# Two transformer blocks on one core: gate columns by TensorE, state steps on POOL, down products by token pair, norm turns emitted later

## The chip, the cores and the metric

The kernel runs on one core of a Trainium2 chip. The metric is device time in microseconds, the median of several runs. TensorE (PE in the profile) multiplies matrices and writes into PSUM; VectorE (DVE), ScalarE (ACT) and GpSimd (POOL) do the elementwise work; SyncE (SP) issues the transfers. Each engine carries out its own instructions in the order in which the program emitted them, and waits on semaphores for the others.

## The reference

Everything is float32, 512 tokens by 1024 features. A first block of two layers and then a second block of two layers are applied. What the change touches is cut out here:

```python
# first block, twice
h = rmsnorm(x, g_pre_mix[l]);  x = x + rmsnorm(token_mixer(h, ...), g_post_mix[l])
h = rmsnorm(x, g_pre_ffn[l]);  x = x + rmsnorm(conv_ffn(h, ...),    g_post_ffn[l])
# token_mixer: chunkwise mLSTM (4 heads, chunks of 128 tokens) beside sliding-window attention
log_i = gates[..., :4];  log_f = log_sigmoid(gates[..., 4:])     # gates: 8 columns per token
bc = cumsum(log_f in the chunk);  m, decays and weights from running maxima of log_i - bc
# conv_ffn: up to 2*2816 features, 3-tap causal convolution, silu(gate)*val, down to 1024
# second block, twice, with a context of 256 tokens
ret_x = bidirectional_retention(...)   # chunks of 128; per chunk: s = s * c_dec + k^T v, both ways
na_x, context_attention, pool_mixer, conv_ffn_2, all modulated by silu(c) @ w_mod
```

The mLSTM gates are 4 input and 4 forget values per token; the recurrence over tokens needs them as rows (one head's 512 tokens along the free axis), and the final division needs two results as columns again (tokens on partitions).

## The kernel before

All products of weights are made of three float32r matmuls (`mm3`, lines 444 to 449): each operand is split into a high part (`wh`, `nh`) and a remainder (`wl`, `nl`). Weights come as slabs of 512 KB through SP into a ring of three raw tiles, ScalarE casts the high part (line 385), VectorE subtracts the remainder (line 386), and five split slabs exist at a time (`NW`). `a_tiles` makes features by tokens (a slab is the stationary operand, up to 512 tokens move), `b_tiles` tokens by features (128 tokens are stationary, 512 weight columns move). Product banks in PSUM (`mm`) are four; four more (`ax`) serve transposes, scores and other small products.

**The order of the work** is laid down by a planned clock. The program is a generator that emits TensorE's products and yields their planned nanoseconds (`6 * 512 / 2.37`, or 1296, for six 512-column matmuls); everything else is put on a heap by `later(delay, fn)` (line 253) and is emitted when the planned clock has passed its due time, that is, at the next yield, in order of due time. Transposes and small products add to the clock themselves (`tr`, line 575: 110 or 60 ns). What is emitted in this order is what each engine runs; the real times follow from the semaphores. `Q` and the `D_` constants are such delays.

**A norm** (`Norm`, lines 124 to 191) goes token tile by token tile: square and sum on ScalarE (line 143), a root by VectorE (570) and a power on POOL (572), scaling of one half by VectorE (154) and of the other by ScalarE (155), then `turn` (159): four transposes each half by TensorE (577), the gain (168, 173, 175), and `put`: high part and remainder into `nh` and `nl` (187, 188). `D_TURN` is the delay from the scaling to the first turn.

**The first block's mixer** (`block1_mix`, line 1224) makes attention's queries (w1q), keys, values and gate columns (w1g), then the mLSTM's queries and keys (w1a, an `a_tiles` of four items, each evicted by ScalarE at line 1243 and finished by three taps on VectorE at line 1246; the last tap frees the bank), its values (w1v, which wants all four banks) and output gate (w1o). Between these products TensorE does the banks of the sliding-window attention (`swa_pair`, line 1027: scores, transposes, copies at 1075 and 1077, values `Q["sw3"]` after the transposes). The gates go their own way: `gates1` (line 892) at `Q["gates"]` after w1g; `gates2` writes them element by element to HBM (912), `gates3` reads them back as rows (920), `gates4` makes the cumulative sum (935), `stab` the running maximum and four more rows (940 to 944), `fin` writes five rows to HBM (950), `cols` reads two of them back as columns, element by element (957), `ends` takes an exponential (962). The mLSTM heads wait for these.

**The FFN** (`ffn`, line 644) is cut into parts by `PARTS1` and `PARTS2`: for each part the up products with convolution, then `down` (line 505): all token tiles for output half 0, then all for half 1. A token is complete when both halves of the last part are in; `b1_sink` then takes the root, updates x and starts the next norm. `down` begins with two tokens and leaves out the last two of the part's feature tiles until both have got the others. Modulation sums of the second block (`mod`, line 795) run on VectorE while an FFN allows it; `keep` (862) writes four gate rows to HBM by 4-byte elements.

**The second block.** `ctx_in` and `x_layer` make the projections, neighbourhood attention, pooling and retention. In `x_layer` the states of the four chunks are chained both ways (line 1861): a step (1353) is a multiply (1357) and an add (1358) over 64 partitions; f steps go to VectorE and b steps to POOL, in turn, the two halves lying in the same tiles. `ret_chunk` (line 1470) then does a chunk: scaling of q (1477), transposes, scores, products with the state. `ctx_attn` (line 1540) normalises its scores on POOL (593) and transposes them `Q["cx2"]` later.

## Time and profile before

| | us |
|---|---|
| median of 3 runs (2811.86 to 2814.61) | 2812.58 |
| the profiled execution, its own time | 2813.32 |
| its span, first to last instruction | 2811.5 |
| TensorE busy | 2705.4 (96%) |
| VectorE busy | 1895.9 (67%) |
| ScalarE busy | 1167.0 (42%) |
| POOL busy | 572.0 (20%) |

The profile is of one execution. A line of it names the source line of the kernel (L447), the engine, the operation and the tiles, "out<-in". A wait is an engine's idle time ahead of an instruction, put down to the semaphore that came last; where two instructions of the other engine end together, the name can be the neighbour's. A matmul's bar is longer than its share of the pipeline: two that follow each other overlap. PEclk is the granted share of TensorE's full clock.

### The profile page before, as it was taken

The numbers are of one execution on the slowest core, as the hardware profiler recorded it, in microseconds if no ns is written. First come the engines' busy times: TensorE is split into PE (matmuls) and PEld (weight loads), VectorE is DVE, ScalarE is ACT, GpSimd is POOL, SyncE is SP. The second block draws the span as 40 slices with busy tenths as digits, with TensorE's granted clock in tenths as the row PEclk, the third lists the DMA queues.
The fourth block names the chain that finished last, engine by engine and source line by source line (L and its number), as shares of the span: only waits on it lengthen the run. The fifth ranks groups of instructions, "written<-read, shape, count | busy, mean of one in ns | idle before, by whom it ended". The sixth has DMA issues, their size and how long they took to land. (4 is left out here: it accounts for less than half of the span.)

```text
span 2811.5 us, 38854 instructions
## 1 busy us (share of the span) xinstructions
PE 2705.4 (96%) x14526; PEld 2291.8 (82%) x14526; DVE 1895.9 (67%) x3414; ACT 1167.0 (42%) x2098; POOL 572.0 (20%) x616
## 2 busy tenths in 40 slices
PE   8899999998999999999999999999999999999998
PEld 6678888876788887788788888888888888888887
DVE  6767777777668678857657787778646556664544
ACT  4555332445554323555443633223336442442433
POOL 2222000042230000234153220221102335201011
PEclk9999999999999999999999999999999999999999
DMA  5633444425334464333332243333513322333332
GB/s 166 89 90 124 148 153 140 145 77 86 91 112 153 149 124 158 123 118 113 105 92 82 87 139 117 105 117 109 87 49 98 116 73 73 97 118 100 98 98 68
DMA packets 135804, 308.22 MB, mean 110 GB/s; under 512 B 38024, under 2 KB 44040, under 8 KB 135616
## 3 DMA queue, kind: packets, MB, share of 16 engines
q1 hardware_dynamic: 135040, 304.69, 37.3%
q8 instruction: 115, 1.88, 0.3%
q10 hardware_dynamic: 576, 1.05, 0.1%
q14 instruction: 73, 0.60, 0.1%
HBM read 303.44 MB, written 2.24 MB: 109 GB/s over the span
## 5 line engine op out<-in xcount | busy, mean ns | idle before, releaser
L385 ACT CAST wh<-wr 128x1024 fp32r<-128x1024 f32 (+2 forms) x455 | 461.3, 1015 | 578.4 <-PE mm L449 259.6
L447 PE MATMUL mm<-nh,wh 128*128 128x512 f32 (+1 forms) x1776 | 671.6, 378 | 3.6 <-DVE nh L187 3.6
L448 PE MATMUL mm<-nl,wh 128*128 128x512 f32 (+1 forms) x1776 | 666.9, 375 | 0.9 <-POOL nl L188 0.4
L449 PE MATMUL mm<-nh,wl 128*128 128x512 f32 (+1 forms) x1776 | 665.9, 375 | 0.0
L386 DVE TENSOR_TENSOR wl<-wr,wh 128x1024 fp32r<-128x1024 f32 (+2 forms) x455 | 572.3, 1263 | 112.5 <-ACT wh L385 112.1
L617 DVE SCALAR_TENSOR_TENSOR u<-mm,vec,u 128x511 f32<-128x511 f32 (+2 forms) x440 | 305.9, 695 | 234.6 <-ACT u L612 163.5
L447 PE MATMUL mm<-wh,u 128*128 128x512 f32 (+1 forms) x1176 | 460.5, 392 | 2.1 <-ACT u L632 1.9
L448 PE MATMUL mm<-wl,u 128*128 128x512 f32 (+1 forms) x1176 | 454.7, 387 | 2.6 <-DVE wl L386 2.4
L449 PE MATMUL mm<-wh,u 128*128 128x512 f32 (+1 forms) x1176 | 454.4, 386 | 2.2 <-DVE u L633 1.5
L447 PEld LDWEIGHTS mm<-nh,wh 128*128 128x128 f32 x1776 | 336.6, 190 | 66.3 <-issue 4.8
L449 PEld LDWEIGHTS mm<-nh,wl 128*128 128x128 f32 x1776 | 336.0, 189 | 60.4
L448 PEld LDWEIGHTS mm<-nl,wh 128*128 128x128 f32 x1776 | 336.6, 190 | 58.1 <-DVE nl L188 1.0
L447 PEld LDWEIGHTS mm<-wh,u 128*128 128x128 f32 x1176 | 221.9, 189 | 46.8 <-ACT u L632 2.7
L449 PEld LDWEIGHTS mm<-wh,u 128*128 128x128 f32 x1176 | 221.6, 188 | 46.0 <-DVE u L633 3.5
L448 PEld LDWEIGHTS mm<-wl,u 128*128 128x128 f32 x1176 | 222.0, 189 | 45.3 <-DVE wl L386 5.0
L447 PE MATMUL mm<-wh,nh 128*128 128x384 f32 (+2 forms) x512 | 191.1, 373 | 17.2 <-DVE t L934 10.8
L577 PE MATMUL ax<-ident,u 128*128 128x128 f32 x930 | 137.4, 283 | 50.6 <-DVE u L154 18.3
L449 PE MATMUL mm<-wh,nl 128*128 128x384 f32 (+2 forms) x512 | 182.0, 355 | 1.5 <-POOL nl L188 1.5
L448 PE MATMUL mm<-wl,nh 128*128 128x384 f32 (+2 forms) x512 | 181.7, 355 | 0.0
L577 PEld LDWEIGHTS ax<-ident,u 128*128 128x128 f32 x930 | 108.5, 144 | 80.9 <-issue 25.0
L737 POOL TENSOR_TENSOR x<-x,u 128x512 f32<-128x512 f32 x64 | 103.2, 1613 | 342.6 <-DVE u L736 341.4
L572 POOL TENSOR_TENSOR t<-t,mhalf 128x1 f32<-128x1 f32 (+2 forms) x76 | 63.3, 835 | 508.1 <-DVE t L570 507.8
(248 smaller groups left out, 3703.9 us busy)
## 6 DMA issues: line engine op xcount, KB each, us to landing
wr<-in_up_dram SPq DMA_DIRECT2D x176, 512.0 KB
mrow<-in_wmod_dram SPq DMA_DIRECT2D x192, 256.0 KB
wr<-in_dn_dram SPq DMA_DIRECT2D x88, 512.0 KB
wr<-in_wo_dram SPq DMA_DIRECT2D x56, 512.0 KB
wr<-in_w2b_dram SPq DMA_DIRECT2D x56, 384.0 KB
wr<-in_w2a_dram SPq DMA_DIRECT2D x39, 512.0 KB
nab<-in_nab_dram SPq DMA_DIRECT2D x36, 128.0 KB
wr<-in_w1q_dram SPq DMA_DIRECT2D x8, 512.0 KB
```

What stands on the lines that cost most here:

```text
L385: nc.scalar.copy(h[:, :n], raw[:, :n])
L386: s.wlo[i] = lambda: nc.vector.tensor_sub(lo[:, :n], raw[:, :n], h[:, :n].bitcast(F32))
L447: mm(ps, ah, bh, start=first, stop=False)
L448: mm(ps, ah, bl, start=False, stop=False)
L449: mm(ps, al, bh, start=False, stop=last)
L572: nc.gpsimd.tensor_tensor(out=r, in0=e, in1=s.mhalf[:, :n], op=ALU.pow)
L577: s.nc.tensor.transpose(out, in_, s.ident[:p, :p])
L617: nc.vector.scalar_tensor_tensor(out=c[:, o], in0=ps[:, i], scalar=w[q], in1=c[:, o], op0=ALU.mult, op1=ALU.add)
L737: eng.tensor_add(x[:, c], x[:, c], o)
```

## The change

Six things, each to be found in the diff:

- `Norm.scale` adds `D_MORE` = 1300 to the delay of both turns, except for the first norm of the kernel.
- `PARTS1` of the first layer becomes (0, 8, 14, 18, 22), as the second layer's is. The last part's down products of both layers of the first block go through a new `down_both`: both halves for tokens 0 and 1, then both for tokens 2 and 3, with all four slabs held.
- `Q["sw3"]` goes from 1250 to 2100 and `Q["cx2"]` from 2160 to 3200.
- `keep` issues its four transfers 4000 ns apart.
- `gates2` turns the gate columns into rows by eight transposes on TensorE, and goes on with what `gates4` did; `fin` writes three rows to HBM where it wrote five, and makes the columns by eight transposes.
- In `x_layer` all six state steps go to POOL, the backward ones first.

```diff
--- before.py
+++ after.py
@@ -29,6 +29,7 @@
 D_SQ = 1080
 D_RSQ = 990
 D_TURN = 1575
+D_MORE = 1300
 D_EV = 1500
 NW = 5
 ALIGNED = ("wh", "wl", "nh", "nl")
@@ -44,11 +45,11 @@
 D_W = 3080
 D_PUMP = 2500
 D_LO = 3000
-PARTS1 = ((0, 8, 16, 22), (0, 8, 14, 18, 22))
+PARTS1 = ((0, 8, 14, 18, 22), (0, 8, 14, 18, 22))
 PARTS2 = ((0, 4, 8, 12, 16, 22), (0, 8, 16, 22))
 CB = ((0, 0), (8, 1), (24, 1), (32, 2))
 NR = 3
-Q = {"swa": 2600, "ctx": 612, "na": 1218, "ret": 6600, "mod": 19000, "mod0": 30000.0, "cn": 18000, "gates": 16000, "fill": 11520, "na1": 1600, "na2": 6253, "na3": 2116, "sw1": 1400, "sw2": 3135, "sw3": 1250, "cx1": 1080, "cx2": 2160, "cx3": 1557}
+Q = {"swa": 2600, "ctx": 612, "na": 1218, "ret": 6600, "mod": 19000, "mod0": 30000.0, "cn": 18000, "gates": 16000, "fill": 11520, "na1": 1600, "na2": 6253, "na3": 2116, "sw1": 1400, "sw2": 3135, "sw3": 2100, "cx1": 1080, "cx2": 3200, "cx3": 1557}
 
 VEC = {}
 NVEC = 0
@@ -125,6 +126,7 @@
     def __init__(n, s, xs, gcol, bcol=None):
         n.s, n.xs, n.g, n.b = s, xs, gcol, bcol
         n.t = len(xs) * P
+        n.first = s.now == 0
         n.done = 0
         n.hh = n.hl = None
 
@@ -153,8 +155,9 @@
         hn = [s.u(), s.u()]
         nc.vector.tensor_scalar(out=hn[0], in0=x[:, :512], scalar1=r, scalar2=None, op0=ALU.mult)
         nc.scalar.activation(hn[1], x[:, 512:], AF.Copy, scale=r)
-        s.later(D_TURN, lambda: n.turn(i, 0, hn))
-        s.later(D_TURN + 426, lambda: n.turn(i, 1, hn))
+        late = 0 if n.first else D_MORE
+        s.later(D_TURN + late, lambda: n.turn(i, 0, hn))
+        s.later(D_TURN + late + 426, lambda: n.turn(i, 1, hn))
 
     def turn(n, i, h, hn):
         s, nc = n.s, n.s.nc
@@ -535,6 +538,35 @@
                     s.drop_w()
             s.done(ev(t, pss[t]))
 
+    def down_both(s, keys, act, ready, ev):
+        ws = [[], []]
+        nk = 2 * len(keys[0])
+        order = [(h, t) for q in ((0, 1), (2, 3)) for h in range(2) for t in q]
+        pss = {}
+
+        def part(n, k0, k1):
+            h, t = order[n]
+            if n not in pss:
+                yield from s.until(lambda: s.free > 0)
+                pss[n] = s.mm()
+            for k in range(k0, k1):
+                if len(ws[h]) <= k // 2:
+                    ws[h].append(s.load_w(keys[h][k // 2]))
+                wh, wl = ws[h][k // 2]
+                c = slice(k % 2 * 512, (k % 2 + 1) * 512)
+                yield from s.until(lambda: ready(k, 0))
+                s.mm3(pss[n], act(k, 0, t), (wh[:, c], wl[:, c]), k == 0, k == nk - 1)
+                if k % 2:
+                    yield 6 * 512 / 2.37
+                    if t == 3:
+                        s.drop_w()
+        for n, (h, t) in enumerate(order):
+            if n == 0:
+                yield from part(0, 0, nk - 2)
+                yield from part(1, 0, nk - 2)
+            yield from part(n, nk - 2 if n < 2 else 0, nk)
+            s.done(ev(h, t, pss[n]))
+
     def down(s, keys, act, ready, tiles, ev):
         w = []
         nk = 2 * len(keys)
@@ -667,6 +699,11 @@
                 c = slice(t * P, (t + 1) * P)
                 return h[:, c], lo[:, c]
             tiles = [(gi, t) for gi, n in enumerate(groups) for t in range(n.t // P)]
+            if up == "up1" and i == np_ - 1:
+                allow(False)
+                keys = [[(dn, (l, h, j)) for j in range(f0 // 2, f1 // 2)] for h in range(2)]
+                yield from s.down_both(keys, act, lambda k, gi, f0=f0: (f0 + k, gi) in g, sinks[0][1])
+                return
             for half in range(2):
                 if half and i == np_ - 1:
                     allow(False)
@@ -861,11 +898,16 @@
 
             def keep():
                 gd = s.dram([2, 2, D], "mgate")
-                for w in range(2):
-                    for i in range(2):
-                        o = (3 * i + 2) * 8
-                        nc.sync.dma_start(gd[w, i].rearrange("(j p) -> p j", p=P), md[:, w, o:o + 8])
-                s.mgate[l] = gd
+
+                def one(n):
+                    w, i = n // 2, n % 2
+                    o = (3 * i + 2) * 8
+                    nc.sync.dma_start(gd[w, i].rearrange("(j p) -> p j", p=P), md[:, w, o:o + 8])
+                    if n < 3:
+                        s.later(4000, lambda: one(n + 1))
+                    else:
+                        s.mgate[l] = gd
+                one(0)
             s.later(1200, keep)
 
         def begin(n):
@@ -902,27 +944,18 @@
         nc.scalar.activation(tmp, tmp, AF.Exp, scale=-1.0)
         nc.scalar.activation(tmp, tmp, AF.Ln, bias=s.one)
         nc.vector.scalar_tensor_tensor(out=lf3, in0=g3[:, :, 4:], scalar=0.0, in1=t3, op0=ALU.min, op1=ALU.subtract)
-        gd = s.dram([8, 512], "grow")
-        s.later(6000, lambda: s.gates2(g3, lf3, gd, got))
-
-    def gates2(s, g3, lf3, gd, got):
-        nc = s.nc
-        for i, src in enumerate((g3, lf3)):
+        s.later(7400, lambda: s.gates2(g3, lf3, got))
+
+    def gates2(s, g3, lf3, got):
+        nc = s.nc
+        rows = []
+        for src in (g3, lf3):
+            ps = s.ax()
             for t in range(NT):
-                nc.sync.dma_start(gd[i * 4:i * 4 + 4, t * P:(t + 1) * P].rearrange("h p -> p h"), src[:, t, :4])
-        s.later(3000, lambda: s.gates3(gd, got))
-
-    def gates3(s, gd, got):
-        nc = s.nc
-        rows = []
-        for i in range(2):
+                s.tr(ps[:4, t * P:(t + 1) * P], src[:, t, :4])
             r = s.u((4, 512))
-            nc.sync.dma_start(r, gd[i * 4:i * 4 + 4])
+            nc.vector.tensor_copy(r, ps[:4, :])
             rows.append(r)
-        s.later(2800, lambda: s.gates4(rows, got))
-
-    def gates4(s, rows, got):
-        nc = s.nc
         li, lfr = rows
         b, bm, m = [s.u((4, 512)) for _ in range(3)]
         a, wi, ws, d0 = li, lfr, b, bm
@@ -942,24 +975,20 @@
             nc.vector.tensor_add(bm, b, m)
             nc.vector.tensor_sub(wi3, mi[:, :NT].unsqueeze(2).to_broadcast([4, NT, P]), m3)
             nc.vector.tensor_sub(ws3, a3, m3[:, :, P - 1:].to_broadcast([4, NT, P]))
-            s.later(2600, fin)
+            s.later(4200, fin)
 
         def fin():
-            gr = s.dram([5, 4, 512], "gfin")
-            for i, x in enumerate((bm, a, m, wi, ws)):
+            gr = s.dram([3, 4, 512], "gfin")
+            for i, x in enumerate((m, wi, ws)):
                 nc.sync.dma_start(gr[i], x)
-            s.later(2600, lambda: cols(gr))
-
-        def cols(gr):
+            ps = s.ax()
+            for i, x in enumerate((bm, a)):
+                for c in range(NT):
+                    o = i * 16 + c * 4
+                    s.tr(ps[:, o:o + 4], x[:, c * P:(c + 1) * P])
             co = s.ti(32)
-            for i in range(2):
-                for c in range(NT):
-                    nc.sync.dma_start(co[:, i * 16 + c * 4:i * 16 + c * 4 + 4],
-                                      gr[i, :, c * P:(c + 1) * P].rearrange("h p -> p h"))
-            s.later(2800, lambda: ends(gr, co))
-
-        def ends(gr, co):
-            nc.scalar.activation(co[:, :16], co[:, :16], AF.Exp, scale=-1.0)
+            nc.scalar.activation(co[:, :16], ps[:, :16], AF.Exp, scale=-1.0)
+            nc.vector.tensor_copy(co[:, 16:], ps[:, 16:32])
             got["gates"] = (co[:, :16], gr, co[:, 16:])
         s.later(1800, stab)
 
@@ -1099,7 +1128,7 @@
         dec = [None] * 4
 
         def bring(hp):
-            for src, dst in ((4, wsb), (3, wib)):
+            for src, dst in ((2, wsb), (1, wib)):
                 w = s.u()
                 for i in range(2):
                     nc.sync.dma_start(w[i * 64:i * 64 + 64, :], gr[src, hp * 2 + i].partition_broadcast(64))
@@ -1108,7 +1137,7 @@
         def bring_m(hp):
             for i in range(2):
                 w = s.u()
-                nc.sync.dma_start(w, gr[2, hp * 2 + i].partition_broadcast(P))
+                nc.sync.dma_start(w, gr[0, hp * 2 + i].partition_broadcast(P))
                 dec[hp * 2 + i] = w
             s.later(2800, lambda: mask(hp))
 
@@ -1859,10 +1888,10 @@
         gn = s.gn_row(l)
         yield from s.in_b(l, 0, norm, s.tok(rq, True))
         yield from s.until(lambda: len(kv) == NT)
+        for d in range(NT - 1, 0, -1):
+            s.step(nc.gpsimd, rc, b, st[d - 1], st[d])
         for c in range(NT - 1):
-            s.step(nc.vector, rc, f, st[c + 1], st[c])
-            d = NT - 1 - c
-            s.step(nc.gpsimd, rc, b, st[d - 1], st[d])
+            s.step(nc.gpsimd, rc, f, st[c + 1], st[c])
 
         def ev_gate(t, ps):
             gate[t] = s.ret_gate1(ps, gn)
```

## Rows read from the trace of the kernel before

**Rows 1.** The page's busy time by engine, and the clock of the core.
```profile
PE 2705.4 (96%) x14526; PEld 2291.8 (82%) x14526; DVE 1895.9 (67%) x3414; ACT 1167.0 (42%) x2098; POOL 572.0 (20%) x616
...
core 0: 2811.5 us, clock 0.989
```
**Rows 2.** TensorE's waits, whole span: us in total, times, longest.
```profile
PE ax L577 <- DVE u L154: 18.3, 12, 7.0
PE mm L447 <- DVE t L934: 10.8, 2, 5.4
PE ax L577 <- DVE u L1477: 10.3, 2, 5.2
PE mm L447 <- DVE nh L187: 9.8, 4, 3.3
PE ax L589 <- ACT u L1075: 7.3, 6, 3.0
...
PE ax L577 <- ACT u L155: 3.7, 2, 2.1
```
**Rows 3.** Timeline of 1481 to 1500, VectorE and POOL: start, us, instruction.
```profile
1487.51 0.95 DVE L1381 TENSOR_TENSOR u<-u,cos 128x384 f32<-128x384 f32 x1
...
1491.79 0.55 DVE L1357 TENSOR_TENSOR u<-u,t 64x384 f32<-64x384 f32 x1 [2.09 <-POOL u L1358]
...
1498.79 1.81 DVE L1477 TENSOR_TENSOR u<-u,t 128x384 f32<-128x384 f32 x2
...
1481.24 6.80 POOL L1379 TENSOR_TENSOR u<-u,sin 128x192 f32<-128x192 f32 x8 [4.92 <-ACT u L1715]
1489.84 0.83 POOL L1357 TENSOR_TENSOR u<-u,t 64x384 f32<-64x384 f32 x1 [1.80 <-DVE u L1358]
1490.75 1.00 POOL L1358 TENSOR_TENSOR u<-u,u 64x384 f32<-64x384 f32 x1
...
1497.40 2.32 POOL L1358 TENSOR_TENSOR u<-u,u 64x384 f32<-64x384 f32 x1
```
**Rows 4.** Timeline of 1494 to 1519, TensorE.
```profile
1500.19 1.54 PE L577 MATMUL ax<-ident,u 128*128 128x128 f32 x6 [5.13 <-DVE u L1477]
...
1508.30 0.42 PE L447 MATMUL mm<-wh,nh 128*128 128x384 f32 x1
...
1513.24 0.82 PE L577 MATMUL ax<-ident,u 128*128 128x128 f32 x6
...
1518.60 0.48 PE L447 MATMUL mm<-wh,u 128*128 128x512 f32 x1
```
**Rows 5.** Stretches: length, busy time (instructions) of each engine, clock, DMA share, GB/s.
```profile
185.00:205.00 20.00, 20.00 (x90) 16.53 (x89) 10.10 (x13) 8.44 (x16) 5.49 (x5) 1.00 0.42 132
226.00:250.00 24.00, 20.18 (x141) 19.15 (x139) 16.22 (x25) 9.07 (x20) 6.96 (x6) 0.86 0.33 99
596.00:610.00 14.00, 8.35 (x36) 6.05 (x35) 11.90 (x21) 10.37 (x22) 8.40 (x8) 0.88 0.12 32
1096.00:1172.00 76.00, 72.33 (x315) 58.63 (x315) 59.13 (x106) 26.75 (x39) 1.53 (x2) 1.00 0.41 136
```
**Rows 6.** Timeline of 98 to 114, lines of TensorE and VectorE.
```profile
101.73 0.77 PE L447 MATMUL mm<-wh,nh 128*128 128x512 f32 x1 [5.38 <-DVE t L934]
...
98.20 0.75 DVE L1246 SCALAR_TENSOR_TENSOR u<-mm,vec,u 128x511 f32<-128x511 f32 x1 [2.22 <-ACT u L1243]
100.84 0.74 DVE L1246 SCALAR_TENSOR_TENSOR u<-mm,vec,u 128x509 f32<-128x509 f32 x1
103.69 1.21 DVE L935 TENSOR_TENSOR_SCAN u<-u,u 4x512 f32<-4x512 f32 x1 [2.11 <-DMA u<-grow]
109.68 1.91 DVE L940 TENSOR_TENSOR_SCAN u<-u,u 4x512 f32<-4x512 f32 x1
112.91 0.67 DVE L944 TENSOR_TENSOR u<-u,u 4x512 f32<-4x512 f32 x1
```
**Rows 7.** TensorE's waits from 1225 to 1270, in the first `ctx_in`.
```profile
PE ax L577 <- POOL u L593: 5.1, 4, 2.2
```

More of the change, by code (lines that the diff above doesn't have):

```diff
@@ L904, in gates1 @@
         nc.vector.scalar_tensor_tensor(out=lf3, in0=g3[:, :, 4:], scalar=0.0, in1=t3, op0=ALU.min, op1=ALU.subtract)
-        gd = s.dram([8, 512], "grow")
-        s.later(6000, lambda: s.gates2(g3, lf3, gd, got))
-    def gates2(s, g3, lf3, gd, got):
-        nc = s.nc
-        for i, src in enumerate((g3, lf3)):
-            for t in range(NT):
-                nc.sync.dma_start(gd[i * 4:i * 4 + 4, t * P:(t + 1) * P].rearrange("h p -> p h"), src[:, t, :4])
-        s.later(3000, lambda: s.gates3(gd, got))
-    def gates3(s, gd, got):
+        s.later(7400, lambda: s.gates2(g3, lf3, got))
+    def gates2(s, g3, lf3, got):
         nc = s.nc
         rows = []
-        for i in range(2):
+        for src in (g3, lf3):
+            ps = s.ax()
+            for t in range(NT):
+                s.tr(ps[:4, t * P:(t + 1) * P], src[:, t, :4])
             r = s.u((4, 512))
-            nc.sync.dma_start(r, gd[i * 4:i * 4 + 4])
+            nc.vector.tensor_copy(r, ps[:4, :])
             rows.append(r)
-        s.later(2800, lambda: s.gates4(rows, got))
-    def gates4(s, rows, got):
-        nc = s.nc
         li, lfr = rows
```

## The prediction

> **What bounds the kernel now.** I read the page's first part and the clock first. TensorE is busy for 2705 of 2811.5 us at a granted clock of 0.989 [rows 1]: about 106 us of idle time and a few slow stretches are all there is to win unless matmuls go, and none go (the reference's products all stay). So only what TensorE waits for matters. The list of its waits [rows 2] is to be read as places: transposes ("ax") of the norms waiting for the scaled token (L154), 18.3 us over 12, of which 7.0 is the kernel's start and 11.3 the other eleven; L155, the same on ScalarE, 3.7; weights products waiting for a normalised token (nh), 9.8 over 4; L1477, the retention chunk, 10.3 in two equal parts; L934, 10.8 in two; L1075, 7.3 over 6. Every layer pays these again, so the two big pairs are one cause each. The sum is made against the profiled execution's own 2813.32 us (span 2811.5 and 1.8 around it); the median of the runs shown is 0.74 lower.
>
> **State steps on POOL (line 1862).** Today the steps alternate: a VectorE step waits 2.09 us for a POOL step on the same tile and the other way round, and only behind the third VectorE step does L1477 come, at 1498.79 [rows 3]; TensorE has stood 5.13 us [rows 4]. Without the steps VectorE has L1381 done at 1488.46 [rows 3]; two adds of a like size, one weight remainder (about 1.2) and L1477 (1.81) follow, so about 1493.4, before TensorE gets there (1500.19 less 5.13). The wait goes. Behind it TensorE ran slower: from the transposes at 1500.19 to the first matmul after the products at 1508.30 is 8.11 us, the next chunk's same instructions take 5.36 (1513.24 to 1518.60) [rows 4]; 2.75 more. Per layer 7.9, for two 15.8; I take off 1.0 for VectorE, which then stands nearer to the chain: **-14.8**. What is late next? POOL does six steps in a row, 0.83 and 1.00 each, from about 1488.0 when its rotary work ends [rows 3]. The backward steps come first, so the state of chunk 0 is there at about 1493.7, and the products, over at 1508.30 today, want it no earlier than about 1498. Every f step lies ahead of its chunk too. POOL's bound is 0.83 and 2.32 a step [rows 3]: third step at 1497.5, still in time.
> That 2.32 us add began while VectorE ran two operations with both inputs in SBUF. The Trainium skill (SBUF — State Buffer, "Who interferes with whom") says that such an operation and a GpSimd one which reads SBUF lock each other out for a whole instruction. The trace agrees: 2.32 against 1.00. By that rule all six steps run at the long price and the state is ready at 1497.5, so it changes neither sign nor sum here.
>
> **Norm turns one step later (D_MORE).** The program is emitted by a planned clock that moves in steps of 1296 (six 512-column products); 1575 falls on the second step, 2875 on the third. So each turn is passed by six more products, 6 x 20/90 = 1.33 us [rows 5], if there are any. Thirteen waits for L154 and L155 (the start excepted) come to 15.0 us, mean 1.15 [rows 2]; one is at the first layer's end, below. For the twelve others I take 0.95 each, 11.4. At both ends of the mixers (226 to 250 in the first layer, idle 3.8 [rows 5], and the second alike) the last token has no products left to hide behind; but its root no longer queues behind the stores of the token ahead: 1.0 each. **-13.4**; bounds 4 (half of the waits only move to nh) and 15.0, and 3 us more if the slow clock of 0.86 at 226 goes.
>
> **Down products by token pair, parts (8, 14, 18, 22).** In the first layer's last down stage token 0 was complete 42 products before the end; now it is 60 of 96, 13.3 us. The 42 were 9.3 us, so its chain has 4.0 us more. TensorE idles 14.0 - 8.35 = 5.65 us there and the clock is 0.88, worth 1.7 [rows 5]; less 4.0 the wait is 1.65, and I leave 2.0 of the 7.4, as tokens 2 and 3 are complete only 12 and 0 products ahead: **-5.4** (0 to 7.4). Against it, the smaller part has twelve products, not 24, before it needs its last activation. The second layer has these very parts, and from 1096 to 1172, over the starts of its last two down stages, TensorE idles 3.7 us [rows 5]: **+3.7**. The eight added partial sums are VectorE work of some 0.75 us each (a tap's price [rows 6]) within one part's up stage and down stage, hidden while VectorE is busy 67% [rows 1]. In the second layer nothing waits for its tokens: 0. Four weight tiles of five are held at once; they were split a tile ahead, and if they weren't, a wait for a remainder is about 1.3 us each. That the modulation sums pause one half earlier costs nothing, since their rows are fetched only in the second block.
>
> **ctx_attn (cx2).** Its four waits for POOL's L593 are 5.1 us [rows 7]; one step later, 1.1 remains, and I give back 1.5 to weights that come no sooner: **-2.4** (0 to 5.1).
>
> **Gates and sw3.** SP loses 16 element-wise transfers and 4 whole ones a layer, and spreads the four of `keep`. No wait of TensorE in the list is put down to a transfer, so 0; were a weight's transfer late behind them, it would be a gain. sw3 takes the value products past one more step: of the 7.3 us for L1075 I take 4.5. But the order on VectorE matters. TensorE stands 5.38 us at 101.73, put down to L934; by the code it is the fourth bank of the value product that it wants, which the third tap (L1246, 100.84 to 101.58) frees; L934 only stands beside it [rows 6]. The change does not remove that. By the planned clock (the yields, transposes and scores of the code added up since w1g) gates1 comes 17288 ns after the w1g products; 7400 more is 24688, inside the point (24622 to 26355) at which a bank's scores and transposes are emitted, and that point comes ahead of the last w1a item's own taps. So gates2 stands before them on VectorE: two copies of 0.75, scan 1.21, a sub of 0.67 and a small copy, some 3.5 us, where VectorE was idle 2.22 ahead of 98.20; +1.3. And the block `stab`, due 1800 after it, falls before the third tap, due 2194 after. It runs from 109.68 to 113.58, 3.9 us [rows 6], and then stands in front of TensorE. The bank waits, and behind that product all of TensorE's queue. The eight transposes of gates2 lie inside this wait; the eight of `fin` don't, 1.1 (six take 0.82 [rows 4]); its exp and 16-column copy are small and awaited only by the mLSTM heads, much later. 6.3 per layer, 12.6 for two, less 4.5: **+8.1**. Bounds: -3 (stab after the tap) and +12 (two more slow windows).
>
> **Sum.** -14.8 - 13.4 - 5.4 + 3.7 - 2.4 + 8.1 = -24.2; 2813.3 - 24.2 - 0.7 = **2788.4 us**.
>
> **Rivals.** (a) *The gates don't stand in the way*: the tap goes first, or another link frees TensorE. The 8.1 becomes about zero: 2780. For it speaks the list, which names L934; against it the planned clock, which gives today's order of VectorE row by row. (b) *Waits that only move*: a turn that comes later finds TensorE at nh or at a weight remainder, because the last token's chain is no shorter. Half of the 13.4 + 5.4 + 2.4 is lost, 10.6: about 2799; all of it, 2809, no measurable change. For it: nh has 9.8 us over 4 already. (c) *Slower*: of the ten norms' 34 tokens each turn is put 1.33 us later, also where the consumer is next in line. Without the 13.4 the sum is -10.8; from 13 such tokens on, at 1.33 each, it is past 2813.3 + 5.6 less the 0.7, and with all 34 it is 2847. Against it: only 4 nh waits in the whole list, so few turns are next in line. (d) *It doesn't do what it says*: 1300 would move nothing if it fell within one step; it doesn't, as worked out.
>
> **Numbers.** Forecast 0.52 (its own range 2779 to 2797), (a) 0.20, (b) 0.22 (0.07 of it within 0.2%), (c) 0.05, (d) 0.01. About 0.2%, 5.6 us, is what a measurement of this kernel can tell from no change. Faster 0.87, same 0.08, slower 0.05. The range 2773 to 2806 takes in the forecast, (a) with two slow windows gone, and most of (b).
>
> **What would show it.** L1477 gone from the waits, six POOL steps in a row from 1488, and the chunk's instructions at the 5.36 us of today's second chunk: the first term right. The first value product of each mixer waiting about 8.5 us, for something behind L944: the gates right; 5.4 or less: rival (a). At the first layer's end idle of about 2 in place of 5.65, and new waits of 3.7 together before its two last down stages. L154 and L155 together under 4 us apart from the start, with nh at 9.8 or less; nh above it is (b) or (c). A wait of the chunk's products for POOL, or for a weight in the pair-wise stage, would prove me wrong there.

## The result and the profile after

The changed kernel takes **2839.6 us** (median of 4 runs, 2836.5 to 2845.8) against 2812.7 before: ratio 1.0098, 95% interval 1.0078 to 1.0117. It is slower by 27 us where 24 less were forecast. The profiled execution is the longest of the four, 2845.8, 6 us above the median, and what is read from it below is of that one execution. Its first page lines and its list of TensorE's waits (engine, operation and line; releaser; us in total, times, longest) answer to [rows 1, 2]:

```profile
core 0: 2844.0 us, clock 0.981
PE 2718.3 (96%) x14558; PEld 2302.0 (81%) x14558; DVE 1899.9 (67%) x3416; ACT 1166.5 (41%) x2098; POOL 587.6 (21%) x628
```

```profile
PE mm L450 <- DVE u L1275: 16.1, 2, 8.1
PE ax L609 <- DVE u L156: 13.0, 7, 6.9
PE mm L450 <- DVE nh L190: 12.0, 4, 5.4
PE mm L450 <- ACT u L664: 10.8, 4, 7.8
PE ax L609 <- DVE u L1506: 10.2, 4, 3.3
PE mm L450 <- DVE u L649: 9.5, 2, 8.7
PE mm L451 <- DVE wl L389: 8.8, 9, 2.7
...
PE ax L613 <- DVE u L1517: 3.8, 2, 1.9
...
PE mm L452 <- DVE wl L389: 2.8, 1, 2.8
PE ax L609 <- POOL u L625: 2.7, 4, 0.9
```

Idle time rose from 106.1 to 125.7 us (span less busy), and busy time by 12.9 with only 32 small transposes more, whose bars are 3.9 us together: behind the longer waits the granted clock is at half of its full rate for longer (0.50 in every microsecond from 1517 to 1523, behind the retention's waits; 0.981 over the span, where 0.989 was). Line numbers have moved (L154 is L156, L187 L190, L386 L389, L632 L664, L617 L649, L593 L625, L1246 L1275, L1477 L1506, L1488 L1517). Read group by group: the norms' L156 fell from 18.3 to 13.0 [rows 2], but L190 rose from 9.8 to 12.0, and the waits for weight remainders (L389) from 4.7 in four to 11.6 in ten. The retention did not lose its 10.3; it has 14.0, now with L1517. The first value product has 16.1 where it had 10.8. Two waits are new: 7.84 for L664 and 8.74 for L649. The largest, from the timelines of the changed kernel (start, us, engine, line, operation, shapes, [idle before it <- releaser]):

```profile
106.23 0.76 PE L450 MATMUL mm<-wh,nh 128*128 128x512 f32 x1 [8.06 <-DVE u L1275]
610.95 0.80 PE L450 MATMUL mm<-wh,nh 128*128 128x512 f32 x1 [5.38 <-DVE nh L190]
1118.93 0.80 PE L450 MATMUL mm<-wh,u 128*128 128x512 f32 x1 [7.84 <-ACT u L664]
1514.78 0.55 PE L609 MATMUL ax<-ident,u 128*128 128x128 f32 x3 [3.31 <-DVE u L1506]
...
2030.56 0.55 PE L450 MATMUL mm<-u,wh 128*128 128x256 f32 x1 [8.74 <-DVE u L649]
```

**Retention.** VectorE's and POOL's timeline at the first of the two places (answers to [rows 3]):

```profile
1513.14 0.98 POOL L1387 TENSOR_TENSOR u<-u,u 64x384 f32<-64x384 f32 x1
1514.16 0.56 DVE L1506 TENSOR_TENSOR u<-u,t 128x384 f32<-128x384 f32 x1 [5.75 <-POOL u L1387]
...
1516.50 0.56 DVE L1506 TENSOR_TENSOR u<-u,t 128x384 f32<-128x384 f32 x1 [1.78 <-POOL u L1387]
1518.84 0.56 DVE L1517 COPY u<-ax 128x384 f32<-128x384 f32 x1 [1.78 <-POOL u L1387]
```

L1506 twice, and the first L1517 behind them, wait for the fourth, fifth and sixth step on POOL. None of them reads a state: L1506 scales q, L1517 copies transposes. The addresses in the built program tell why (first layer of the second block):

```
step 4 (L1386, L1387): temporary at 51712     first  L1506 writes to 51712
step 5               : temporary at 43520     second L1506 writes to 43520
step 6               : temporary at 45568     first  L1517 writes to 45568
```

The temporary of a step is taken from the common ring `u` and given back after the add, and a buffer that was given back soon goes out again to another tile, here to VectorE's next three. The second layer shows the same pattern. In the kernel before, all six temporaries of a layer lie at one address, 72192.

**The gates.** At the first value product, VectorE does the block `stab` (L973 to L977) and then the third tap, and TensorE goes on at 106.23:

```profile
102.21 1.20 DVE L973 TENSOR_TENSOR_SCAN u<-u,u 4x512 f32<-4x512 f32 x1
...
105.36 0.73 DVE L1275 SCALAR_TENSOR_TENSOR u<-mm,vec,u 128x509 f32<-128x509 f32 x1
```

**The two new waits.** SP and ScalarE before 1118.93, and VectorE before 2030.56:

```profile
1049.84 2.56 SPq L374 DMA_DIRECT2D wr<-in_up_dram  x2
1052.45 0.73 SPq L905 DMA_DIRECT2D mgate<-md  x1
...
1073.43 0.86 SPq L374 DMA_DIRECT2D wr<-in_up_dram  x2
...
1063.83 1.05 ACT L388 CAST wh<-wr 128x1024 fp32r<-128x1024 f32 x1 [10.99 <-DMA wr<-in_up_dram]
...
1082.94 0.68 ACT L642 ACTIVATE u<-mm,vec 128x512 f32<-128x512 f32 x1
...
2027.63 0.75 DVE L872 CUSTOM_DVE_ANT_0 junk<-mrow,crow,macc 128x512 bf16<-128x512 f32 x1 [7.64 <-DMA mrow<-in_wmod_dram]
...
2029.42 0.99 DVE L649 SCALAR_TENSOR_TENSOR u<-mm,vec,u 128x255 f32<-128x255 f32 x2
```

No weight's transfer is issued from 1052.4 to 1073.4. Weights and modulation rows share SP's queue with `keep`'s writes, and an mrow fetch that waits for its buffer, which a modulation sum has yet to read, holds up the weights behind it. SP waits 18.9 us in two for sums in this stretch, the longest time 12.0; in the kernel before it is 10.6 in four. A cast of the kernel before in the same stage:

```profile
1053.82 1.05 ACT L385 CAST wh<-wr 128x1024 fp32r<-128x1024 f32 x1 [15.14 <-DMA wr<-in_up_dram]
```

ScalarE stands at its casts, 26.0 us at four of them; in the kernel before one cast there waits 15.14 us, longer than any of these, but the four only 18.3 together. The first convolution step of the part (L642) comes at 1082.94, 52.0 us after the last one of the part ahead (41.9 in the kernel before), and from 1083.65 VectorE has no idle time until after 1118. The length of this gap goes with the stall in all the kernels run here: 39.2 to 43.6 us with a stall of 1.0 (the kernel before, runs 4, 5, 6, 10, 11 and 12), 46.5 to 46.8 with 3.9 to 4.1 (runs 1, 2 and 9), 49.1 to 52.0 with 5.5 to 7.8 (the changed kernel, runs 3, 7 and 8). So the chain from late slabs to TensorE is seen; which edit makes the slabs late is another question, for runs 1 and 2.

Before 2030.56 VectorE does one modulation sum after the other, with no convolution between, and stands 7.64 us for the row of the last two: the planned clock has reached the last part of the second block's first FFN, where the program waits until both layers' gate rows are issued, and emits all that is left of the modulation at once.

### The profile page after: what moved, and what is told of

Same layout as the page of the kernel before. It is cut to its first block, busy times and chain, and to the rows that moved or that the text cites. A ratio compares the mean times of both kernels' runs of the same rounds, so it can differ in the third digit from the quotient of the medians.

```text
span 2844.0 us, 38890 instructions
## 1 busy us (share of the span) xinstructions
PE 2718.3 (96%) x14558; PEld 2302.0 (81%) x14558; DVE 1899.9 (67%) x3416; ACT 1166.5 (41%) x2098; POOL 587.6 (21%) x628
## 4 chain that ended last, share of the span: by engine, by line
PE 80%; DVE 8%; ACT 3%; POOL 3%; DMA 2%; issue 2%; SPq 0%; POOLq 0%; ACTq 0%; DVEq 0%
PE mm L450 24%; PE mm L451 24%; PE mm L452 24%; PE ax L613 4%; PE ax L609 3%; DVE wl L389 2%; PE ax L621 1%; DMA wr<-in_up_dram 1%; ACT wh L388 1%; ACT u L178 1%; DVE junk L872 1%; DVE u L649 0%; POOL u L1386 0%; POOL t L604 0%; DMA mrow<-in_wmod_dram 0%
## 5 line engine op out<-in xcount | busy, mean ns | idle before, releaser
L389 DVE TENSOR_TENSOR wl<-wr,wh 128x1024 fp32r<-128x1024 f32 (+2 forms) x455 | 577.0, 1273 | 102.6 <-ACT wh L388 100.7
L450 PE MATMUL mm<-wh,u 128*128 128x512 f32 (+1 forms) x1176 | 461.7, 393 | 10.8 <-ACT u L664 10.8
L649 DVE SCALAR_TENSOR_TENSOR u<-mm,vec,u 128x511 f32<-128x511 f32 (+2 forms) x440 | 306.0, 696 | 240.4 <-ACT u L644 160.8
L450 PE MATMUL mm<-wh,nh 128*128 128x384 f32 (+2 forms) x512 | 192.4, 376 | 24.2 <-DVE u L1275 16.1
L609 PE MATMUL ax<-ident,u 128*128 128x128 f32 (+1 forms) x946 | 137.1, 280 | 37.3 <-DVE u L156 13.0
L609 PEld LDWEIGHTS ax<-ident,u 128*128 128x128 f32 (+1 forms) x946 | 109.5, 144 | 66.2 <-issue 18.4
```

What stands on the lines that cost most here:

```text
L389: s.wlo[i] = lambda: nc.vector.tensor_sub(lo[:, :n], raw[:, :n], h[:, :n].bitcast(F32))
L450: mm(ps, ah, bh, start=first, stop=False)
L609: s.nc.tensor.transpose(out, in_, s.ident[:p, :p])
L649: nc.vector.scalar_tensor_tensor(out=c[:, o], in0=ps[:, i], scalar=w[q], in1=c[:, o], op0=ALU.mult, op1=ALU.add)
```

## The experiments

Each kernel was run with the kernel before beside it; "from the changed kernel" and "from the kernel before" say what was edited. "Less" and "more" are against the median of the kernel that was edited. The changed kernel's own four runs lie 9.3 us apart (2836.5 to 2845.8) and are those of the result: a difference of about 5 us from their median is at the edge of what they can show, and its size is uncertain by several us.

**1. Keep at once** (from the changed kernel).

```diff
-                    if n < 3:
-                        s.later(4000, lambda: one(n + 1))
...
-                one(0)
+                for n in range(4):
+                    one(n)
+                s.mgate[l] = gd
```

> The changed kernel, with the four gate transfers of keep issued together again. Theory (spread writes): the two new stalls of the changed kernel, 7.84 us at 1111.10 and 8.74 us at 2021.81, come from the spreading: in the first the four writes of 4-byte elements slow the weight transfers for longer, ScalarE stands at a cast and VectorE's convolutions fall behind; in the second the last part waits for the gate rows, which are announced only with the fourth write. Then the first goes back to about 2.1 (as in the kernel before) and the second under 1: 13 us of idle time and some 3 us of slow clock less, about 2824. Rival (paused sums): the sums of the modulation are late because they now pause over the whole down stage by token pairs; then the second stall stays and the time is about 2832 to 2840.

Measured: 2834.3 us (2829.3 to 2835.6), 5.4 less. The first stall is 4.07, the second 5.58, so neither went, and the rival fits the time. Nor can it be said that both shrank: in the traces of runs 3, 7, 8 and 9, which leave `keep` and the pause as they are in the changed kernel, the first is 4.0 to 7.7 and the second 3.6 to 6.5. What spreading costs by itself stays open.

**2. Pause half way** (from the changed kernel): `allow(False)` moves into `down_both`, ahead of the fifth of its eight products.

```diff
-                allow(False)
...
+            if n == 4:
+                pause()
```

> The changed kernel, with the modulation's sums paused only from the fifth of the eight products of the stage by token pairs (half way, about where the kernel before pauses them) and not from its start. Theory (paused sums): the sums fall behind in the two stages, so that the last part of the second block's first FFN overtakes them; with the shorter pause they end earlier, and the second new stall (8.74, in other runs 5.5 to 6.5) goes to under 1, and the first (7.84) to about 2: about 2826. Rival (spread writes alone): both stalls stay where keep is still spread, 4 to 8 us each, and the time is 2836 to 2842.

Measured: 2834.9 us (2832.0 to 2835.4), 4.8 less. The second stall is gone: the list of waits from 1600 to 2160 has no row at all, with `keep` still spread. The first is 3.91, again just under the lowest of the runs that undo neither. So the longer pause makes the second. Of the first it can be said that it is 1.0 where both are undone (run 11, with other edits); its shares are not shown, and the long pause without spread writes goes with 4.07 in run 1 and with 1.0 in run 10.

**3. A scratch tile for the steps** (from the changed kernel): one tile, of the tag that the norms' discarded squares use, serves all six steps of a layer.

```diff
+        t = s.junk().bitcast(F32)
         for d in range(NT - 1, 0, -1):
-            s.step(nc.gpsimd, rc, b, st[d - 1], st[d])
+            s.step(nc.gpsimd, rc, b, st[d - 1], st[d], t)
...
```

> The changed kernel, with the six state steps of a layer using one scratch tile of their own in place of six from the common ring of buffers; all on POOL as before. Theory (buffers): VectorE's scaling of q (L1506) and its copy (L1517) wait for POOL only because they are given the buffers that the last three steps' temporaries held; then TensorE's 3.31 + 1.79 + 1.90 at 1511 and at 2382 go, and the slow clock behind them (6.8 and 17.1 us at half speed) with them: 14 + about 10, near 2816. Rival (data): the chunk's products need the states, and six steps of some 2.3 us each are too long whichever buffer they use: the same 7 us reappear at L613, and the time stays at 2836 to 2842.

Measured: 2818.2 us (2813.5 to 2821.2, 10 runs), 21.4 less. TensorE's only wait of the stretch 1480 to 1530 in the list of waits, and the two L1506 in the timeline:

```profile
PE ax L613 <- DVE u L1517: 0.3, 1, 0.3
```

```profile
1505.25 2.48 DVE L1506 TENSOR_TENSOR u<-u,t 128x384 f32<-128x384 f32 x2
```

The buffers were the wait; the data come in time, as the prediction had it.

**4. The same scratch tile in the kernel before**, its forward steps on VectorE, its backward ones on POOL, each in its own half of the partitions.

```diff
+        t = s.junk().bitcast(F32)
         for c in range(NT - 1):
-            s.step(nc.vector, rc, f, st[c + 1], st[c])
+            s.step(nc.vector, rc, f, st[c + 1], st[c], t)
...
```

> The kernel before, its steps still alternating between VectorE (forward) and POOL (backward), but with one scratch tile for all of a layer's steps, forward steps in its one half of the partitions and backward steps in the other. Theory (buffers): the steps took turns (2.09 us of waiting each) only because each took the buffer that the step ahead of it had just left; now neither engine waits for the other, VectorE's three steps end about 3.5 us after they start, TensorE's 5.13 and 5.16 us go and the slow transposes behind them: 2 x 7.9 less, near 2797. Rival (data): the two chains meet in the state tiles and must take turns: the waits stay and the time is 2812.

Measured: 2809.6 us (2807.0 to 2816.4, 10 runs), ratio 0.9995 (0.9985 to 1.0005). A miss, and an instructive one. No step waits for the other engine any more, so the 2.09 us of [rows 3] were the shared temporary; yet TensorE still stands 3.19 us. The timeline:

```profile
1489.61 1.03 POOL L1357 TENSOR_TENSOR junk<-u,t 64x384 f32<-64x384 f32 x1
1489.87 1.18 DVE L1357 TENSOR_TENSOR junk<-u,t 64x384 f32<-64x384 f32 x1
1490.71 1.21 POOL L1358 TENSOR_TENSOR u<-u,junk 64x384 f32<-64x384 f32 x1
1491.08 1.25 DVE L1358 TENSOR_TENSOR u<-u,junk 64x384 f32<-64x384 f32 x1
...
1499.12 1.01 DVE L1477 TENSOR_TENSOR u<-u,t 128x384 f32<-128x384 f32 x2
```

VectorE's instructions take 1.07 to 1.26 us, not the 0.55 of [rows 3]; its three steps take 7.3 us.

**5. All six steps on VectorE**, with the scratch tile, backward first (from the kernel before).

```diff
+        t = s.junk().bitcast(F32)
+        for d in range(NT - 1, 0, -1):
+            s.step(nc.vector, rc, b, st[d - 1], st[d], t)
...
```

> The kernel before with all six steps on VectorE and one scratch tile. In the run with the steps on both engines side by side each VectorE instruction took 1.07 to 1.26 us where it takes 0.55 with POOL at rest. Theory (lock-out: two engines at work on SBUF take turns, so the second one gains nothing): twelve instructions of 0.55 us on VectorE alone end no later than the two chains side by side, 6.6 us against 7.3, and TensorE's wait is 2.5 to 3.2 us as there: 2805 to 2809. Rival (the slow instructions of that run had another cause): the twelve take 13 us and the waits grow to 8 us or more: 2820.

Measured: 2813.3 us (2805.9 to 2815.8, 10 runs), so the time is not what was expected, but the order on VectorE is: twelve instructions from 1490.05 to 1497.04, and TensorE's wait is 3.00 at both places. In the execution traced, a longer slow stretch took back what the shorter waits gave: the granted clock from 1495 to 1512 is 0.65 here (the column before the last two), 0.80 in the kernel before and 0.90 in run 4.

```profile
1490.05 0.56 DVE L1357 TENSOR_TENSOR junk<-u,t 64x384 f32<-64x384 f32 x1
...
1496.49 0.55 DVE L1358 TENSOR_TENSOR u<-u,junk 64x384 f32<-64x384 f32 x1
...
1499.04 1.01 DVE L1477 TENSOR_TENSOR u<-u,t 128x384 f32<-128x384 f32 x2
```

```profile
1495.00:1512.00 17.00, 13.97 (x66) 12.77 (x65) 11.14 (x20) 2.18 (x5) 0.00 (x0) 0.65 0.31 93
```

Six steps on VectorE alone end with the three that it does beside POOL (L1477 at 1499.04 and 1499.12): the second engine gained nothing.

**6. All six on POOL**, with the scratch tile (from the kernel before): run 5 with `nc.gpsimd` for `nc.vector`.

> The kernel before with only the state steps changed: all six on POOL, backward first, as in the change, but with one scratch tile of their own. Theory (buffers): this is the term of the prediction without the reuse of buffers that spoiled it; VectorE goes on to L1477 at once, the waits of 5.13 and 5.16 us and the slow transposes behind them go: 15 less, 2798, though VectorE's own instructions run longer beside POOL's (2.5 us for the two of L1477 in the repaired changed kernel, against 1.0). Rival (lock-out): those longer instructions keep L1477 late, 2 to 3 us of each wait stay, 2806.

Measured: 2799.3 us (2798.5 to 2802.4), ratio 0.995 (0.9935 to 0.9965), 13.5 less. This is the term of the prediction, 14.8, without the reuse of buffers. VectorE's L1477 takes 2.47 for two here, and TensorE's only wait from 1480 to 1520 is 0.3:

```profile
1495.23 2.47 DVE L1477 TENSOR_TENSOR u<-u,t 128x384 f32<-128x384 f32 x2
```

```profile
PE ax L581 <- DVE u L1488: 0.3, 1, 0.3
```

**7. Gates behind the tap** (from the changed kernel).

```diff
-        s.later(7400, lambda: s.gates2(g3, lf3, got))
+        s.later(12500, lambda: s.gates2(g3, lf3, got))
```

> The changed kernel, with gates2 due 12500 ns after gates1 in place of 7400, so that its copies, its scan and stab are all emitted behind the third tap. Theory (order on VectorE): TensorE's 8.06 and 8.04 us at the first value product are the third tap behind stab; both go back to about 5.4, 5.3 us less in all, near 2834. Rival (gates late): the mLSTM heads wait for the gates, and what is won returns as idle time before their products: 2838 to 2845. If the 8 us stay, the wait was not for the tap.

Measured: 2834.6 us (2833.2 to 2835.8), 5.0 less:

```profile
100.29 0.77 PE L450 MATMUL mm<-wh,nh 128*128 128x512 f32 x1 [5.11 <-DVE u L1275]
```

The order on VectorE set the wait, as predicted: 16.1 falls to 10.2 in the two layers. Waits for L444 come later, 2.4 for two, 1.11 of them here. It is L1275, the tap, that is named also now, as the prediction read the 5.38 of before, which stood under L934 [rows 6].

**8. No later turns** (from the changed kernel).

```diff
-D_MORE = 1300
+D_MORE = 0
```

> The changed kernel with D_MORE = 0. Theory of the prediction (turns): the waits for L156 and L157 come back, some 11 us more, near 2850. Rival (waits that move): L156 and L157 come back, but the waits for nh (12.0 us over 4, the 5.38 at the first layer's end among them) and for weight remainders (11.6 us over 10, most at norms) shrink by as much: 2835 to 2843. If the wait at the first layer's end (5.96) falls to about 2, D_MORE is what spoiled the stage by token pairs there.

Measured: 2834.4 us (2827.4 to 2837.0), 5.2 **less**. Its waits, and the first layer's end:

```profile
PE ax L609 <- DVE u L156: 17.5, 11, 6.9
...
PE mm L450 <- DVE nh L190: 8.2, 4, 2.6
```

```profile
608.55 0.50 PE L450 MATMUL mm<-wh,nh 128*128 128x512 f32 x1 [2.04 <-DVE nh L190]
...
620.81 1.09 PE L609 MATMUL ax<-ident,u 128*128 128x128 f32 x8 [1.96 <-DVE u L156]
```

L156 comes back by 4.5 and L157 by 2.5, but nh falls by 3.8, nearly all of it at this one place (5.38 to 2.04, against which stands the 1.96 behind it), and the waits for remainders fall from 11.6 to 4.7, what they were before the change. Some of the 5.2 need not be D_MORE's: in this run's trace the two stalls are 5.5 and 4.8, too.

**9. The exception mended** (from the changed kernel): `n.first` is true for the kernel's first norm alone.

```diff
-        n.first = s.now == 0
+        n.first = s.now == 0 and gcol is s.gfirst
...
```

> The changed kernel, with the exception from D_MORE for the kernel's first norm alone. As written the exception asks whether the planned clock is zero, and the first layer's FFN norm is made at that time too, so its turns were never moved. Theory: now the waits for L156 at 216, 235 and 243 (0.67, 0.96 and 0.90) and nh's 1.79 shrink as the second layer's did (4.8 to 3.3 there): 1 to 2 us less, 2838. Rival: nh or a weight remainder takes their place in full: no change.

Measured: 2837.7 us (2833.5 to 2839.4), 1.9 less, within what the runs scatter. In the waits from 210 to 250, L156's 2.5 in three and nh's 1.8 become nh's 2.2, 1.1 for weight remainders and 0.3 for nl: 0.7 us less.

**10. Only the stage by token pairs and the parts** (from the kernel before): `down_both`, its call and `PARTS1` as in the change's diff.

> The kernel before with only the last down stages of the first block by token pairs and the new parts of its first layer. Theory of the prediction: the wait at the first layer's end falls from 5.65 to about 2, and two waits of about 1 each come before the last two down stages: 2811. Rival (VectorE's queue): the first token's remainder still stands on VectorE behind the roots and updates of the tokens that now end close behind it, so the 5.65 stay and the time is 2815; and where the sums are paused longer, a stall of 5 us or more comes near 1990 to 2000: 2820 to 2825.

Measured: 2820.2 us (2816.5 to 2825.4), ratio 1.0029 (1.0016 to 1.0041), 7.4 more.

```profile
602.25 0.79 PE L447 MATMUL mm<-wh,nh 128*128 128x512 f32 x1 [2.04 <-DVE nh L187]
614.50 1.09 PE L606 MATMUL ax<-ident,u 128*128 128x128 f32 x8 [0.95 <-DVE u L154]
...
2006.55 0.36 PE L447 MATMUL mm<-u,wh 128*128 128x256 f32 x1 [3.24 <-DVE u L646]
```

The wait at the layer's end is 2.63 (2.0 were predicted, and the first theory is right there), with 0.95 for a later token behind it; the parts cost 1.04 twice, and 0.7 in two small waits; and the pause brings a stall of 3.24 at 2006. All this is little in sum: TensorE's idle time rose by only 1.3 us, and its busy time by 5.3 for the same matmuls, at a granted clock of 0.987 where 0.989 was.

**11. All repairs together**, pairs kept: runs 1, 2, 3 and 7, and D_MORE as an argument `late` of three norms alone.

```diff
+        nf = Norm(s, xs, s.v("g_pre_ffn", l, 0, 8), late=D_MORE)
...
+        hold["x"] = Norm(s, xs, *s.mcol(1, 0, 0), late=D_MORE)
```

> The changed kernel with every repair that the runs suggest, the stage by token pairs kept: scratch tile for the steps, gates2 at 12500, keep's four writes at once, the sums paused half way through the stage, and D_MORE for the FFN norms and the second x layer's first norm alone. If the costs are separate, their sum holds: 21.4 (steps), 5.0 (gates), 5.4 (keep), 4.8 (pause) and about 6 (D_MORE) off 2839.6, about 2797. If two of them were paying for the same idle time (keep and pause at 1111 and 2021), it is 2802 or more.

Measured: 2794.9 us (2792.5 to 2795.7), ratio 0.9931 (0.9916 to 0.9945). The single costs, 21.4 + 5.4 + 4.8 + 5.0 + 5.2 = 41.8, are near the 44.7 that went, though the four small ones are uncertain and the last is of another edit (no later turns at all).

**12. The same without pairs and new parts**: run 11 with `down`, its pause and `PARTS1` of the kernel before.

> The same repairs, but the first block's last down stages and parts as in the kernel before, so that neither the parts (two waits of 1.04) nor the longer pause is paid. Against the kernel before: steps 15 less, ctx_attn's transposes 3, sw3 and the gates 3 to 4, the turns of three norms 5 less: about 2786. If the stage by token pairs is worth its 3 us at the first layer's end, the kernel above it is as fast.

Measured: **2787.2 us** (2785.3 to 2788.0), ratio 0.9903 (0.9887 to 0.992): faster than both kernels, by 25.6 and 52.4 us. That this is next to the forecast of 2788.4 is chance: it has other edits and other terms. Its core:

```profile
core 0: 2785.6 us, clock 0.992
```

Pairs and parts together cost 7.7 us against it, though the pause is mended: at the parts' seams in the first layer run 11 idles 4.5 us (from 500 to 590 TensorE is busy 85.5 of 90; here in the same stretch all 90), and its layer's end, 0.90 + 2.04 + 2.35, is hardly better than 1.52 + 0.79 + 3.27 here.

## Why the prediction was wrong

| term | predicted | measured | from |
|---|---|---|---|
| state steps | -14.8 | +7.9 (-13.5 and +21.4 for the buffers) | runs 6, 3 |
| later turns | -13.4 | +5.2, uncertain | run 8 |
| pairs and parts | -5.4 + 3.7 | +7.4 | run 10 |
| keep | 0 | +5.4, uncertain | run 1 |
| gates and sw3 | +8.1 | +6.1 (2.2 of waits, 3.9 of transposes), before any slow clock | lists of waits, bars |
| ctx_attn | -2.4 | -4.2 | lists of waits |

The measured column sums to +27.8, and 27.0 were there; so close a match is partly luck, since the rows come from runs of different kernels, which share some idle time, and two of them are uncertain. No run has sw3, cx2 or the gate columns alone. Terms taken from lists of waits: the value product +5.3, L1078 and L1104 together 7.8 where L1049 and L1075 had 10.9; L593's 6.9 to L625's 2.7.

**State steps: "so about 1493.4, before TensorE gets there ... The wait goes."** This step failed, and with it most of the forecast: where 14.8 less was said, the state steps made the kernel about 8 slower. It took VectorE's queue for the only thing between it and L1477. L1477 writes a buffer, and who read that buffer last was not asked; L1506, as it is now, stood 5.75 and 1.78 us for POOL's fourth and fifth step. What was said of POOL held in kind: the steps went in a row, at about 2.3 us each, between the 1.9 of the text and its bound of 3.15, which by the rule it cites all six should have paid, and were in time for the products (0.3 us of waiting in run 3). The slow clock made the loss larger: granted clock (the column before the last two) in the stretches behind the two waits, from the windows of the changed kernel:

```profile
1508.00:1524.00 16.00, 8.99 (x52) 7.81 (x50) 5.84 (x9) 2.01 (x3) 10.11 (x10) 0.79 0.24 65
2380.00:2404.00 24.00, 16.98 (x79) 15.70 (x78) 8.77 (x15) 3.58 (x5) 9.04 (x10) 0.64 0.22 66
```

**Turns: "each turn is passed by six more products ... For the twelve others I take 0.95 each".** No gain came, and run 8 points to a loss. L156 and L157 did fall, from 15.0 to 7.3 beside the start, less than the 11.4. But the sum had no term for what comes behind a turn: its evictions and `put` stand on VectorE behind the next tokens' roots and updates, so a turn that is 1.3 us later can leave nh later by more. At the first layer's end the gain (L171) is done at 605.6, and ahead of nh stand a root, a weight remainder and an update; with D_MORE = 0 nh comes at 607.01:

```profile
609.14 1.42 DVE L761 SCALAR_TENSOR_TENSOR x<-u,t,x 128x512 f32<-128x512 f32 x2 [0.43 <-POOL t L604]
610.47 0.42 DVE L190 CAST nh<-u 128x512 fp32r<-128x512 f32 x1
```

There it cost 3.34 (5.38 against 2.04; less the 1.96 that a later token then waits), which is rival (c) at one place; remainders took 6.9 more (11.6 against 4.7), which is rival (b). The first layer's FFN norm was not moved at all, since it is made while the planned clock is still zero; I had counted it, and rival (d) should have been looked for in the exception.

**Pairs: "I leave 2.0 of the 7.4 ... +3.7 ... That the modulation sums pause one half earlier costs nothing, since their rows are fetched only in the second block."** The first figure was right alone (2.63 in run 10, with 0.95 behind it), the second of the right size (2.8 at the two seams in run 10, 4.5 in run 11). The third is the failed step: the pause cost a stall of 3.24 in run 10 and of 3.6 to 8.7 wherever the changed kernel kept it. That the rows are fetched only in the second block is not what counts: the code wants all the sums before the last part of the second block's first FFN, and the pause was not made up by then. No row of the kernel before showed a wait there, but it had little time left: its last sum ends at 1996.21, and the part's first convolution step on VectorE follows at 1996.52.

**Keep: "No wait of TensorE in the list is put down to a transfer, so 0".** The cover was not named. It is the stock of split slabs, and ScalarE's and VectorE's lead over TensorE: in the kernel before it covers a wait of 15.14 for a slab, and in the changed kernel the four waits of 26.0 reach TensorE at 1111, under the name of L664, 58 us after the first of them began. So the list of TensorE's waits could not tell how near the cover was to its end. Whether spreading the writes costs anything by itself is not shown (run 1).

**Gates** were right in mechanism and place: the wait is 8.06 and 8.04, behind L977 and the tap, and goes back with the order (run 7). The "about 8.5" is luck: the terms of the sum, 1.3 and 3.9 on top of 5.38, make 10.6. The tap ends 4.5 us later than before (106.09 against 101.58), but TensorE, too, comes to the product 1.8 later (95.87 against 94.03), since the eight transposes of gates2 stand ahead of the product and not inside the wait, as was said; 2.7 of the wait are left, and the transposes are paid beside it. **ctx_attn** gained more than its middle value (whose own terms make 2.5, not 2.4), within its bounds.

The range left out the buffers, the pause and what comes behind a turn: an edit or a side of one that was priced at nothing or asked only for its gain.

## What to carry to other kernels

Before a step is moved off a busy engine, follow its temporaries: where a common ring soon hands a returned buffer out again, a scratch tile joins its user to what is emitted next, and a private tile can be worth more than the move (21.4 us here, where the move gained 13.5). A delay put on one link of a chain has to be followed to the consumer through every queue that it joins again. Background work that pauses must make up its time before someone asks for the result; find that place first.

## What the runs showed of the hardware

For these steps VectorE and POOL side by side gained nothing over VectorE alone. A step (multiply and add, both inputs in SBUF, 64 by 384) takes VectorE 1.17 us alone (run 5) and 2.4 us beside POOL's (run 4), POOL's instructions starting in turn with VectorE's. The Trainium skill (SBUF — State Buffer, "Who interferes with whom") says that a VectorE instruction with two SBUF inputs contends with a GpSimd one that reads SBUF; the trace agrees, 0.56 against 1.07 to 1.26 us, and with all steps on POOL (run 6) VectorE's L1477 takes 2.47 beside them, against 1.01 for two.

Writes of 4-byte elements took long for their size. `keep`'s four, 4 KB each, took 14.5 us from issue to landing in the changed kernel (median, 1040 to 1085), where a modulation row of 256 KB took 7.6:

```profile
mrow<-in_wmod_dram SPq DMA_DIRECT2D x4, 256.0 KB, 7.6
...
mgate<-md SPq DMA_DIRECT2D x4, 4.0 KB, 14.5
```
